# First modulation weights moved ahead of the small loads, the small loads on ScalarE's queue, and another order of the first products

## The chip, the cores and the metric

The kernel runs on one core of one Trainium2 chip. The metric is the device time of one execution in microseconds; the program is launched once and does all four layers. TensorE has two clock levels, 1.2 and 2.4 GHz; the profile gives the granted level as a share of the higher one.

## The reference, cut to what matters

Four layers of a decoder are computed for 256 prompt rows and 32 sample rows, 288 rows together, in float32. Each sub-layer's input is modulated by a shift and a scale per sequence, which come from a product of the condition vectors with a weight of 1024 x 6144 per layer. Layer 0 begins with the gated MLP mixer.

```python
    sc = jax.nn.silu(c)
    for i in range(DEPTH):
        mod = sc @ prm['w_ada'][i] + prm['b_ada'][i]
        sh1, sc1, g1, sh2, sc2, g2 = jnp.split(mod[:, None, :], 6, axis=-1)
        h = x * (1 + sc1) + sh1
        if kind == 0:
            out, v_rows = chunk_mlp_mixer(h, prm['a_w_in'][j], ...)   # z = gelu(h @ w_in)
        x = layer_norm(ALPHA * x + g1 * out, prm['ln1_g'][i], prm['ln1_b'][i])
```

So nothing of layer 0 can be multiplied with its first weight before the condition rows, the first third of `w_ada[0]` and the rows of x are there.

## The kernel before, in words

Activations lie transposed, as eight slices of 128 features x 288 rows. Each float32 product is made of three products of a rounded high part and a low part (`mm3`: Hi x hi at L294, Hi x lo at L295, Lo x hi at L297), so every weight is split on its way: ScalarE copies the high part (`hi`, L240), VectorE subtracts it (`lo`, L241), both 1024 columns at a time. Weights stream from HBM through five 1 MB buffers (`raw`); `set_plan` holds the order of the loads, `advance` and `reach` issue the next load as soon as a buffer is free, and `pump_` splits. A scheduler of the language then sets the order on each engine from the program's text, its priorities and the `issue_after` fences. Every engine executes its list strictly in that order.

The start of the program, which the change touches, goes in these steps (`setup`):

- Eight small loads on SyncE's queue (SP): the condition rows `crow` (two loads), constants `con` (identity and a selection matrix), biases `vb` (two), the prompt rows `xr` (two of 512 KB) and the sample rows `xs`. Then come the first loads of the plan. A load's completion is counted on one of eight semaphores, handed out in turn over the loads of all hardware queues, so a load waits until the eighth load before it has landed. GpSimd's queue (POOL) issues ten further small loads at the same time (`late_loads`).
- Transposes on TensorE: `crow` (L399), `vb` (L405, L406), then x slice by slice (two of `xr` at L413, one of `xs` at L414), copied out of PSUM by VectorE (L415). The SiLU of the condition is `scT`.
- The first third of the modulation in two halves (`ada_first`, g = 0 and 1). A half has four weight tiles of 1 MB, each in two loads of 512 KB and each worth four matmuls with 512 columns (L558). Each matmul writes another 32 rows of one PSUM bank. Then ScalarE copies the bank (L564, `adas`), TensorE gathers it with four small matmuls (L567), and VectorE adds the bias and makes the shift B and the scale A (L572, L573).
- `h_stream` makes Hi and Lo of four slices per half (ScalarE L705 and L708, VectorE L706 to L714).
- The first four output tiles of the value half of `a_w_in` are accumulated together (`run_units` with `inter`): for each of the eight slices k, twelve matmuls over the four tiles. `s.after(k + 1)` holds the products of slice k until a certain modulation matmul has been issued; the list `paced` holds the last matmul of g = 0 and then one for each of the four tiles of g = 1.

Of the kernel before, what the change touches and what calls it, by code (L numbers as in the profile page):

```python
# [56 lines left out]
class Net:  # L57
# [256 lines left out]
    def run_units(s, keys, x, evac, m0=0, nk=8, inter=False, kgroups=1, quiet=False):  # L314

        npair = len(keys) // kgroups
        done = 0
        pair = 0
        if inter:
            ks = keys[:2]  # L320
            ws = [s.get(k) for k in ks]
            pss = [s.psmm() for _ in range(4)]
            for k in range(nk):
                if k < nk - 1:
                    for part in range(2):
                        for m in range(4):
                            with s.after(k + 1):
                                s.mm3(pss[m][:, :T], s.wtile(ws[m // 2], k, m % 2), x(k), k == 0, False, (part,))
                    continue
                for m in range(4):  # L330
                    with s.after(k + 1):
                        s.mm3(pss[m][:, :T], s.wtile(ws[m // 2], k, m % 2), x(k), False, True)
                    if m % 2:
                        s.wfree(ks[m // 2])
                    evac(m0 + m, pss[m])
            s.paced = []
            pair = 2
        while pair < npair:
            if quiet and pair == npair - QPAIR:
                s.quiet = bool(QUIET)  # L340
            pss = [s.psmm() for _ in range(2)]
            for g in range(kgroups):
                key = keys[pair * kgroups + g]
                w = s.get(key)
                for m in range(2):
                    for k in range(nk):
                        s.mm3(pss[m][:, :T], s.wtile(w, k, m), x(g * nk + k), g == 0 and k == 0,
                              g == kgroups - 1 and k == nk - 1)
                    if m == 1:
                        s.wfree(key)  # L350
                    if g == kgroups - 1:
                        evac(m0 + pair * 2 + m, pss[m])
            pair += 1


    def setup(s):
        nc, I = s.nc, s.I
        c = s.cst
        ncst = I["consts"].shape[1]
        s.con = c.tile([128, ncst], F32, name="con")  # L360
        o = CONST_OFF
        cv = lambda k: s.con[:, o[k][0]:o[k][0] + o[k][1]]
        s.cv = cv
        s.id = cv("ident")
        s.onesD = cv("onesD")
        s.ones128 = cv("ones128")
        s.scT = c.tile([128, 8, 32], F32, name="scT")
        s.modT = [c.tile([128, 48, 9], F32, name=f"modT{i}") for i in range(2)]
        s.vT1 = c.tile([128, 128], F32, name="vT1")
        s.vT2 = c.tile([128, 128], F32, name="vT2")  # L370
        s.bT = c.tile([128, 192], F32, name="bT")
        s.X0 = s.acp.tile([128, NCH, T], F32, name="Z", tag="Z")
        s.AX = s.acp.tile([128, NCH, T], F32, name="AX")
        s.Hi = s.acp.tile([128, NCH, T], R32, name="Hi")
        s.Lo = s.acp.tile([128, NCH, T], R32, name="Lo")
        s.A = [s.acp.tile([128, 8, 9], F32, name=f"A{i}") for i in range(2)]
        s.B = [s.acp.tile([128, 8, 9], F32, name=f"B{i}") for i in range(2)]
        i0 = s.layers[0]
        with s.tc.tile_pool(name="ld", bufs=1) as ld:
            crow = ld.tile([9, D], F32, name="crow")  # L380
            vb = [ld.tile([96, 128], F32, name=f"vb{i}") for i in range(2)]
            xr = [ld.tile([128, D], F32, name=f"xr{i}") for i in range(2)]
            xs = ld.tile([32, D], F32, name="xs")

            nc.sync.dma_start(crow[0:1, :], I["c_prompt"])
            nc.sync.dma_start(crow[1:9, :], I["c_sample"])
            nc.sync.dma_start(s.con[:, :146], I["consts"][:, :146])
            bsrc = I["b_ada"].rearrange("l (c p) -> (l c) p", p=128)
            for i in range(2):
                nc.sync.dma_start(vb[i], bsrc[96 * i:96 * i + 96, :])  # L390
            for i in range(2):
                nc.sync.dma_start(xr[i], I["x_prompt"][0, 128 * i:128 * i + 128, :])
            nc.sync.dma_start(xs, I["x_sample"].rearrange("b t d -> (b t) d"))
            s.advance()

            nc.vector.memset(s.scT, 0.0)
            pt = s.psx()
            for k in range(8):
                nc.tensor.transpose(pt[:, 9 * k:9 * k + 9], crow[:, 128 * k:128 * k + 128], s.id[:9, :9])  # L399
            sg = s.wrk.tile([128, T], F32, name="sg", tag="hf", bufs=4)  # L400
            s.act(sg[:, :72], pt[:, :72], AF.Sigmoid)
            nc.vector.tensor_tensor(s.scT[:, :, :9], sg[:, :72].rearrange("p (k n) -> p k n", k=8),
                                    pt[:, :72].rearrange("p (k n) -> p k n", k=8), op=OP.mult)
            pt = s.psx()
            nc.tensor.transpose(pt[:, 0:96], vb[0], s.id[:96, :96])  # L405
            nc.tensor.transpose(pt[:, 96:192], vb[1], s.id[:96, :96])  # L406
            nc.vector.tensor_copy(s.bT, pt[:, :192])

            each = s.h_stream(s.X0, 0)
            for ch in range(NCH):  # L410
                pt = s.psx()
                for i in range(2):
                    nc.tensor.transpose(pt[:, 128 * i:128 * i + 128], xr[i][:, 128 * ch:128 * ch + 128], s.id)  # L413
                nc.tensor.transpose(pt[:, 256:288], xs[:, 128 * ch:128 * ch + 128], s.id[:32, :32])  # L414
                nc.vector.tensor_copy(s.X0[:, ch, :], pt[:, :T])  # L415
            for g in range(2):
                s.ada_first(i0, g)
                for ch in range(4 * g, 4 * g + 4):
                    each(ch)
                if g == 0:  # L420
                    s.late_loads()

# [1434 lines left out]
```

## Time and profile before

| | before |
|---|---|
| median of 3 runs | 1615.36 us (1612.78 to 1615.41) |
| the profiled execution, its own time | 1613.43 us |
| its span | 1611.7 us |
| TensorE matmul busy | 1566.9 us (97%) |
| VectorE, ScalarE busy | 1025.4 us (64%), 798.8 us (50%) |
| DMA | 332.60 MB, mean 206 GB/s |

The profile is of one execution. Its span is the time between the first and the last instruction; 1.7 us of that execution's own time lie around it. Matmuls are pipelined, so a busy TensorE is not a TensorE at its peak. Times in the trace count from the span's start.

### The profile page before, as it was taken

To read this page: it belongs to the slowest core of one execution; us is meant where nothing else is said; L and a number is where in the kernel's file an instruction comes from. 1 tells how busy PE (TensorE), PEld (TensorE's weight loads), DVE (VectorE), ACT (ScalarE), POOL (GpSimd) and SP (SyncE) were. 2 spreads that over 40 slices of the span, in tenths; PEclk is the share of its full clock that TensorE was granted. 3 is DMA by queue.
4 is the path that set the end of the run, shared out by engine and by line. 5 is a ranking of instruction groups with operands and counts; after the bars stand their busy time and mean duration, and the time that the engine had idled before them with its cause. 6 is when DMAs were issued, how large, how long until landed. Compare 5 with 4: busy or idle time off the path is not lost.

```text
span 1611.7 us, 30562 instructions
## 1 busy us (share of the span) xinstructions
PE 1566.9 (97%) x12538; PEld 1399.0 (87%) x12538; DVE 1025.4 (64%) x2290; ACT 798.8 (50%) x1435; POOL 53.1 (3%) x70
## 2 busy tenths in 40 slices
PE   7999899999999999999999999999999999999997
PEld 3778699998889789999987776779999888899997
DVE  3559564557777797556586445496565785964655
ACT  2555453545777656345354444455354463653542
POOL 1000000000001000000002110000000000000000
PEclk9999999999999999999999999999999999999999
DMA  9977695557745878554565455777545675755431
GB/s 333 341 254 242 220 293 160 163 175 246 227 142 163 276 277 280 166 174 159 162 230 186 144 184 212 259 268 240 172 157 173 245 236 192 230 191 176 157 106 43
DMA packets 222718, 332.60 MB, mean 206 GB/s; under 512 B 7171, under 2 KB 196041, under 8 KB 213362
## 3 DMA queue, kind: packets, MB, share of 16 engines
q1 hardware_dynamic: 215954, 299.86, 55.7%
q0 software_dynamic: 6624, 30.78, 5.7%
q8 instruction: 99, 1.62, 0.4%
q14 instruction: 41, 0.34, 0.1%
HBM read 324.09 MB, written 6.53 MB: 205 GB/s over the span
## 4 chain that ended last, share of the span: by engine, by line
PE 87%; DVE 6%; DMA 4%; ACT 2%; issue 1%; SPq 0%; POOL 0%; DVEq 0%; ACTq 0%; POOLq 0%
PE mm L294 23%; PE mm L297 23%; PE mm L295 22%; PE ada L504 3%; PE mm L1456 2%; DMA raw<-in_ffn_w 1%; DVE lo L241 1%; PE mx L1474 1%; PE mm L1510 1%; DVE Z L674 1%; PE mx L1528 1%; DMA raw<-in_a_w_in 1%; PE mx L863 1%; PE mx L1478 1%; PE mx L965 1%
## 5 line engine op out<-in xcount | busy, mean ns | idle before, releaser
L241 DVE TENSOR_TENSOR lo<-raw,hi 128x1024 fp32r<-128x1024 f32 x360 | 433.5, 1220 | 179.2 <-ACT hi L240 179.0
L240 ACT ACTIVATE hi<-raw 128x1024 fp32r<-128x1024 f32 x360 | 371.1, 1052 | 268.4 <-PE mm L297 194.2
L294 PE MATMUL mm<-Hi,hi 128*128 128x288 f32 x1064 | 316.5, 301 | 10.2 <-ACT hi L240 6.2
L295 PE MATMUL mm<-Hi,lo 128*128 128x288 f32 x1064 | 314.5, 299 | 0.5 <-DVE lo L241 0.4
L297 PE MATMUL mm<-FL,hi 128*128 128x288 f32 x1024 | 303.6, 297 | 0.0
L294 PE MATMUL mm<-FH,hi 128*128 128x288 f32 x1024 | 302.6, 296 | 0.0
L295 PE MATMUL mm<-FH,lo 128*128 128x288 f32 x1024 | 298.6, 292 | 0.0
L297 PE MATMUL mm<-Lo,hi 128*128 128x288 f32 x1064 | 296.4, 297 | 0.0
L294 PEld LDWEIGHTS mm<-Hi,hi 128*128 128x128 f32 x1064 | 200.1, 188 | 30.8 <-issue 10.9
L294 PE MATMUL mm<-OH,hi 128*128 128x288 f32 x704 | 206.6, 298 | 1.4 <-ACT OH L705 1.2
L295 PE MATMUL mm<-OH,lo 128*128 128x288 f32 x704 | 205.7, 296 | 0.5 <-DVE lo L241 0.5
L295 PEld LDWEIGHTS mm<-Hi,lo 128*128 128x128 f32 x1064 | 200.4, 188 | 5.9 <-issue 2.5
L297 PEld LDWEIGHTS mm<-Lo,hi 128*128 128x128 f32 x1064 | 193.9, 189 | 6.7 <-issue 5.9
L295 PEld LDWEIGHTS mm<-FH,lo 128*128 128x128 f32 x1024 | 195.2, 191 | 0.0
L297 PE MATMUL mm<-OL,hi 128*128 128x288 f32 x704 | 195.1, 295 | 0.0
L294 PEld LDWEIGHTS mm<-FH,hi 128*128 128x128 f32 x1024 | 192.4, 188 | 0.0
L297 PEld LDWEIGHTS mm<-FL,hi 128*128 128x128 f32 x1024 | 191.9, 187 | 0.0
L294 PEld LDWEIGHTS mm<-OH,hi 128*128 128x128 f32 x704 | 131.8, 187 | 6.9 <-issue 3.4
L784 ACT ACTIVATE r<-mm 128x288 f32<-128x288 f32 x128 | 52.0, 411 | 169.3 <-PE mm L297 163.7
L295 PEld LDWEIGHTS mm<-OH,lo 128*128 128x128 f32 x704 | 132.2, 188 | 1.7 <-issue 0.8
L297 PEld LDWEIGHTS mm<-OL,hi 128*128 128x128 f32 x704 | 128.0, 188 | 1.0 <-issue 0.8
L786 DVE TENSOR_TENSOR s<-r 128x288 f32<-128x288 f32 x128 | 57.7, 455 | 99.6 <-ACT r L784 99.4
(434 smaller groups left out, 2043.7 us busy)
## 6 DMA issues: line engine op xcount, KB each, us to landing
raw<-in_ffn_w SPq DMA_DIRECT2D x128, 1024.0 KB, 5.5
raw<-in_w_ada SPq DMA_DIRECT2D x88, 1024.0 KB, 6.6
raw<-in_a_w_in SPq DMA_DIRECT2D x16, 1024.0 KB, 7.8
raw<-in_b_w_in SPq DMA_DIRECT2D x16, 1024.0 KB, 5.8
raw<-in_w_ada SPq DMA_DIRECT2D x16, 512.0 KB, 9.8
raw<-in_a_w_out SPq DMA_DIRECT2D x8, 1024.0 KB, 7.9
St<-in_state_hgrn POOLq DMA_DIRECT2D x8, 512.0 KB, 5.7
out_hs_s<-St POOLq DMA_DIRECT2D x8, 512.0 KB, 4.4
```

The lines of the kernel that those rows point to most:

```text
L240: nc.scalar.activation(hi[:, a:b], r[:, a:b], AF.Copy)
L241: nc.vector.tensor_tensor(lo[:, a:b], r[:, a:b], hi[:, a:b].bitcast(F32), op=OP.subtract)
L294: mm(out, w[0], x[0], start=first, stop=False)
L295: mm(out, w[1], x[0], start=False, stop=False)
L297: s.last_mm = mm(out, w[0], x[1], start=False, stop=last).ins
L504: nc.tensor.matmul(s.pa[32 * j:32 * j + 32, :], x, w, start=(k == 0), stop=(k == last), skip_group_check=True)
L674: sub = lambda c: nc.vector.tensor_tensor(Z[:, c, :], Z[:, c, :], pm[:, :T], op=OP.subtract)
L784: nc.scalar.activation(r, ps[:, :T], AF.Relu)
L786: nc.vector.tensor_tensor(sq, r, r, op=OP.mult)
L863: nc.tensor.matmul(pt[:, 128 * q:128 * q + 128], vt01[:, q, sl], s.wsT[:, c, :], start=True, stop=True)
L965: mm(pt[32 * b:32 * b + 32, 64 * hh + 32 * g:64 * hh + 32 * g + 32], k[:, hh, a:a + 32], q[:, hh, a:a + 32], start=True, stop=True, skip_g ...
L1456: tr(pt[:, 128 * n:128 * n + 128], lat[b][t // 8][:, t % 8, 128 * c:128 * c + 128], s.id)
```

## The change

The first loads of the plan (`s.advance()`) are issued on SP before anything else, and the eight small loads go to ScalarE's queue. While g = 0 is prepared, splitting is held back (`quiet`), but for two pieces of 1024 columns that are asked for by hand after slices 0 and 2. `s.after(k)` takes the place of `s.after(k + 1)`, so the products of slice k may stand one modulation matmul earlier. Later lines move by seven: what is L558 before is L565 after, L567 is L574, L413 and L414 are L414 and L415, L705 is L712.

```diff
                     for part in range(2):
                         for m in range(4):
-                            with s.after(k + 1):
+                            with s.after(k):
                                 s.mm3(pss[m][:, :T], s.wtile(ws[m // 2], k, m % 2), x(k), k == 0, False, (part,))
                     continue
                 for m in range(4):
-                    with s.after(k + 1):
+                    with s.after(k):
                         s.mm3(pss[m][:, :T], s.wtile(ws[m // 2], k, m % 2), x(k), False, True)
...
-            nc.sync.dma_start(crow[0:1, :], I["c_prompt"])
-            nc.sync.dma_start(crow[1:9, :], I["c_sample"])
-            nc.sync.dma_start(s.con[:, :146], I["consts"][:, :146])
+            s.quiet = True
+            s.advance()
+            nc.scalar.dma_start(crow[0:1, :], I["c_prompt"])
+            nc.scalar.dma_start(crow[1:9, :], I["c_sample"])
+            nc.scalar.dma_start(s.con[:, :146], I["consts"][:, :146])
             bsrc = I["b_ada"].rearrange("l (c p) -> (l c) p", p=128)
             for i in range(2):
-                nc.sync.dma_start(vb[i], bsrc[96 * i:96 * i + 96, :])
+                nc.scalar.dma_start(vb[i], bsrc[96 * i:96 * i + 96, :])
             for i in range(2):
-                nc.sync.dma_start(xr[i], I["x_prompt"][0, 128 * i:128 * i + 128, :])
-            nc.sync.dma_start(xs, I["x_sample"].rearrange("b t d -> (b t) d"))
-            s.advance()
+                nc.scalar.dma_start(xr[i], I["x_prompt"][0, 128 * i:128 * i + 128, :])
+            nc.scalar.dma_start(xs, I["x_sample"].rearrange("b t d -> (b t) d"))
...
             for g in range(2):
+                s.quiet = g == 0
                 s.ada_first(i0, g)
                 for ch in range(4 * g, 4 * g + 4):
                     each(ch)
+                    if g == 0 and ch in (0, 2):
+
+                        s.reach(s.wlist[0])
+                        s.pump_(True)
+                s.quiet = False
```

The order of the instructions differs in the first 560 or so of TensorE's, the first 50 of ScalarE's and the first 36 of VectorE's; behind that all lists are the same. Three places matter.

The first place is the very start of ScalarE's list after the change, with the semaphores that each instruction waits for (DMAHW numbers the eight load semaphores):

```order
L387 DMA crow<-in_c_prompt 1x1024
L388 DMA crow<-in_c_sample 8x1024
L389 DMA con<-in_consts 128x146
L392 DMA vb_97<-in_b_ada 96x128
L392 DMA vb_98<-in_b_ada 96x128
L394 DMA xr_99<-in_x_prompt 128x1024 [waits DMAHW0_49]
L394 DMA xr_100<-in_x_prompt 128x1024 [waits DMAHW2_49]
L395 DMA xs<-in_x_sample 32x1024 [waits DMAHW4_49]
L281 ACT_TABLE_LOAD
L281 ACTIVATE sg<-mx 128x72 [waits PE_49]
```

Before, this list began with the table load. The semaphores now alternate between the two queues; on SP the fourth 512 KB load of `w_ada` waits for the first to land, the fifth for the second and the sixth for the third, where before the eight waited for the eight small loads.

The second place is TensorE's list from the third-last slice of x to the end of g = 0. Before:

```order
L414 MATMUL mx<-con,xs 128x32
L558 MATMUL ada<-raw,scT 32x512
L413 MATMUL mx<-con,xr_99 128x128
L413 MATMUL mx<-con,xr_100 128x128
L414 MATMUL mx<-con,xs 128x32
L413 MATMUL mx<-con,xr_99 128x128
L413 MATMUL mx<-con,xr_100 128x128
L414 MATMUL mx<-con,xs 128x32
L558 MATMUL ada<-raw,scT 32x512 x15
L567 MATMUL mx<-con,adas 128x18 x4
```

And after the change, where one more matmul of the half stands by itself behind slice 2, further up:

```order
L414 MATMUL mx<-con,xr_99 128x128
L414 MATMUL mx<-con,xr_100 128x128
L415 MATMUL mx<-con,xs 128x32
L565 MATMUL ada<-raw,scT 32x512 x4
L414 MATMUL mx<-con,xr_99 128x128
L414 MATMUL mx<-con,xr_100 128x128
L415 MATMUL mx<-con,xs 128x32
L414 MATMUL mx<-con,xr_99 128x128
L414 MATMUL mx<-con,xr_100 128x128
L415 MATMUL mx<-con,xs 128x32
L565 MATMUL ada<-raw,scT 32x512 x11
L574 MATMUL mx<-con,adas 128x18 x4
```

The sixteen matmuls of g = 0 stand as 1 and 15 before and as 1, 4 and 11 after.

The third place is TensorE's list around the end of g = 1. Before, six products of slice 3 stand ahead of the small gathering matmuls and six behind them; then slice 4 begins:

```order
L558 MATMUL ada<-raw,scT 32x512 x4
L294 MATMUL mm<-Hi,hi 128x288
L295 MATMUL mm<-Hi,lo 128x288
L294 MATMUL mm<-Hi,hi 128x288
L295 MATMUL mm<-Hi,lo 128x288
L294 MATMUL mm<-Hi,hi 128x288
L295 MATMUL mm<-Hi,lo 128x288
L567 MATMUL mx<-con,adas 128x18 x4
L445 MATMUL mx<-con,v_259 128x128
L446 MATMUL mx<-con,v_260 128x128
L294 MATMUL mm<-Hi,hi 128x288
L295 MATMUL mm<-Hi,lo 128x288
```

After the change all 48 products of slices 0 to 3 are done when the last modulation matmul is, and the row behind the two transposes is already of slice 4:

```order
L565 MATMUL ada<-raw,scT 32x512 x2
L297 MATMUL mm<-Lo,hi 128x288 x3
L565 MATMUL ada<-raw,scT 32x512 x2
L574 MATMUL mx<-con,adas 128x18 x4
L452 MATMUL mx<-con,v_253 128x128
L453 MATMUL mx<-con,v_254 128x128
L294 MATMUL mm<-Hi,hi 128x288
```

The first products moved the other way: before, the first four matmuls of g = 1 stand ahead of them; after, six products of slice 0 stand ahead of those four matmuls. On ScalarE the first split (L240) now stands between `adas` and the first Hi, where before all four splits stood behind the four slices' Hi and hf.

## Rows read from the trace of the kernel before

**Rows 1.** The page: span, busy time of each engine, one costly group.
```profile
span 1611.7 us, 30562 instructions
PE 1566.9 (97%) x12538; PEld 1399.0 (87%) x12538; DVE 1025.4 (64%) x2290; ACT 798.8 (50%) x1435; POOL 53.1 (3%) x70
L241 DVE TENSOR_TENSOR lo<-raw,hi 128x1024 fp32r<-128x1024 f32 x360 | 433.5, 1220 | 179.2 <-ACT hi L240 179.0
```

**Rows 2.** Chain that ended last, 0 to 60 us: start us, us, what.
```profile
3.37 5.66 DMA xr<-in_x_prompt
...
24.62 0.60 ACT Hi L705
```

**Rows 3.** Timeline of SP's queue: start us, us, what it issues.
```profile
0.81 0.35 SPq L385 DMA_DIRECT2D crow<-in_c_prompt  x1
...
3.84 0.43 SPq L393 DMA_DIRECT2D xs<-in_x_sample  x1
4.31 6.09 SPq L142 DMA_DIRECT2D raw<-in_w_ada  x8
```

**Rows 4.** DMA issues in the stretch 2.55 to 3.05: KB, us to landing.
```profile
xr<-in_x_prompt SPq DMA_DIRECT2D x1, 512.0 KB, 4.4
vb<-in_b_ada SPq DMA_DIRECT2D x1, 48.0 KB, 3.4
...
v<-in_ln_b POOLq DMA_DIRECT2D x1, 16.0 KB, 3.3
```

**Rows 5.** DMA issues in the stretches 3.55 to 4.0 and 5.51 to 6.0.
```profile
xr<-in_x_prompt SPq DMA_DIRECT2D x1, 512.0 KB, 5.7
xs<-in_x_sample SPq DMA_DIRECT2D x1, 128.0 KB, 5.9
...
v<-in_ln_b POOLq DMA_DIRECT2D x1, 16.0 KB, 5.7
...
v<-in_b_lb POOLq DMA_DIRECT2D x1, 16.0 KB, 6.1
```

**Rows 6.** Busy time by stretch: last columns are clock, DMA share, GB/s.
```profile
2.00:3.00 1.00, 0.00 (x0) 0.00 (x0) 0.00 (x0) 0.10 (x1) 1.00 (x3) 1.00 0.57 136
...
4.00:5.00 1.00, 1.00 (x9) 0.97 (x9) 0.00 (x0) 0.08 (x1) 1.00 (x3) 1.00 0.44 83
...
11.00:14.00 3.00, 3.00 (x10) 1.34 (x10) 1.81 (x5) 0.00 (x0) 0.00 (x0) 1.00 1.05 387
...
27.70:31.00 3.30, 2.88 (x8) 0.40 (x8) 2.27 (x4) 3.30 (x5) 0.00 (x0) 0.50 1.05 387
```

**Rows 7.** Timeline of TensorE, 12 to 24 us.
```profile
13.34 1.92 PE L558 MATMUL ada<-raw,scT 128*32 128x512 f32 x2
15.19 0.69 PE L413 MATMUL mx<-con,xr 128*128 128x128 f32 x2
...
16.05 0.69 PE L413 MATMUL mx<-con,xr 128*128 128x128 f32 x2
...
16.91 5.57 PE L558 MATMUL ada<-raw,scT 128*32 128x512 f32 x30
```

**Rows 8.** TensorE groups in 0 to 20.5, 28 to 31, 31.2 to 42.
```profile
L558 PE MATMUL ada<-raw,scT 128*32 128x512 f32 x22 | 6.2, 1023 | 0.0
L558 PE MATMUL ada<-raw,scT 128*32 128x512 f32 x8 | 3.1, 1047 | 3.9 <-DMA raw<-in_w_ada 3.9
L558 PE MATMUL ada<-raw,scT 128*32 128x512 f32 x26 | 6.3, 636 | 0.0
```

**Rows 9.** Timeline of TensorE, 36 to 46 us.
```profile
38.27 1.05 PE L558 MATMUL ada<-raw,scT 128*32 128x512 f32 x4
39.26 0.40 PE L294 MATMUL mm<-Hi,hi 128*128 128x288 f32 x1
...
42.04 0.40 PE L294 MATMUL mm<-Hi,hi 128*128 128x288 f32 x1
...
45.19 0.37 PE L294 MATMUL mm<-Hi,hi 128*128 128x288 f32 x1 [0.18 <-DVE hf L710]
```

## The prediction

> **What bounds the kernel now.** I read the page first. TensorE is busy 97% of the span [rows 1], so almost everywhere its own work sets the pace, and the change leaves that work alone behind the first 560 instructions or so. What it can move is the start. Whatever the start gains or loses until TensorE runs without gaps is carried to the end one for one, because the lists behind are the same. So I followed the chain of waits through the first 60 us. It begins with the load of x: the chain stands on `xr` for 5.66 us, then runs through TensorE's transposes and the modulation matmuls into ScalarE's first Hi [rows 2]. The reader is to see that the chain goes through **x, not through the modulation weights**. `xs` is issued at 3.84 and lands 5.9 us later, at 9.7 [rows 3, 5], and from there TensorE has hardly a pause until the sixteen modulation matmuls of g = 0 end at 16.91 + 5.57 = 22.5 [rows 7]. I call that moment G. The products of slice 4, the first that need g = 1, start at 45.19 [rows 9]. From there the program is the same in both kernels, so the start of slice 4 is my yardstick.
>
> **The change, part by part.** *Issue of the weights.* They begin at 0.81 in place of 4.31, 3.5 us earlier [rows 3]. That is no gain by itself: TensorE reaches the weights behind the transposes of x, and no row there waits for a weight of g = 0 [rows 7]. I set it to zero. Its cover is x; if x came at once, the weights would be next.
>
> *Landing of x.* This is the large term. The trace has no load on ScalarE's queue, so I take the nearest: the small loads on POOL's queue, which run against SP's queue at the same time. A 16 KB load issued near 2.6 lands 3.3 us later, and SP's `vb` from the same half microsecond 3.4 later [rows 4]. Another 16 KB load lands after 5.7 us, and the 512 KB `xr` beside it after 5.7 as well; a later one still takes 6.1 [rows 5]. A load of a thirtieth of the size lands when the large one does, so the two queues **take turns load by load**, one of mine against one of yours, whatever their sizes. ScalarE's queue has eight loads: five small ones, two `xr`, then `xs`. Against each now stands a 512 KB load of weights. SP's queue does not run dry, although its fourth load waits for the first to land: two more are still queued then. So `xs` comes behind seven of the weight loads. At 387 GB/s [rows 6] one of these (524288 bytes) takes 1.35 us, seven 9.5. The three loads of x (1.18 MB) take 3.0. The small loads kept the DMA engines busy for 0.57 us between 2 and 3 and 0.44 between 4 and 5 [rows 6]; for all of them I take 1.5. Transfers start at about 2.1 (none before 2, 136 GB/s in the next microsecond). Sum: 2.1 + 9.5 + 3.0 + 1.5 = 16.1, say 16.3, against 9.7: **+6.6 us**. Bounds: 0, if ScalarE's loads lose nothing, and 8.0, if all eight weight loads go ahead. I take the value near the upper end, because the rows of POOL's queue are the only ones with two queues at once. The Trainium skill (DMA: Bandwidth & Descriptors, Issuing engines are not separate DMA queues) holds that loads from several issuing engines interleave on the same DMA engines and that a second issuer saves no more than the time to issue; by that sentence alone x would lose only its share of the bandwidth, the term would be +1.1 (the first rival) and the sum +3.3. The same page (Queues, rings and completion order) adds that an engine drains a whole packet of one queue before it turns to the next; by that the term stays at +6.6, and the trace agrees for POOL's and SP's queues, while no run here shows ScalarE's. The table load on ScalarE comes behind the eight issues and the condition's transposes behind `con`; both end long before 16.3, so I cost them at zero.
>
> *The order of the sixteen matmuls.* At this point TensorE runs at its lower level. The granted column holds 1.00 here, but the durations decide: L558 takes 1023 ns on average before 20.5, as in the stretch with 0.50 granted (1047), and 636 where 1.00 is granted later [rows 6, 8]. Up to four neighbours of these matmuls run side by side, so one alone costs as much as a group. The single one took 15.19 - 13.34 = 1.85 us [rows 7]. Before: 1.85 + 5.57 = 7.4, the last part of it at the full level. After, as 1, 4 and 11: 1.85 + 1.85 + three groups of 1.7 to 1.85, say 5.3, sum 9.0: **+1.6 us**. The six slices of x in between cost 0.86 each in either order (16.05 - 15.19). Bounds: -0.6, if the level rises ahead of the eleven and halves them (2.2 less), and 1.8.
>
> *From G to slice 4.* Before: 45.19 - 22.5 = 22.7. After, three edits go together. The early split puts the first products before the matmuls of g = 1. Hi begins 2.1 behind G as before [rows 2], then lo (1.2 [rows 1]) and the first Lo follow, so I estimate that the matmuls of g = 1 start at G + 5.0, where before they waited 3.9 us for weights [rows 8] and started at G + 5.6: -0.6. Those weights are now early, since G is late. Then TensorE has the first four together (1.0), six pairs at 0.99 (39.26 - 38.27 [rows 9]), 42 products at about 0.134 (5.6) and some 1.0 for going back and forth: 13.5. The last piece, from the end of g = 1 to slice 4, is 45.19 - 42.04 = 3.15 [rows 9]. It held twelve products before and holds none now, which is what `s.after(k)` gives back of its gain. Sum at the full level 5.0 + 13.5 + 3.15 = 21.7. The pause behind G lets the level fall as it did before (0.50 in 27.70:31.00 [rows 6]). That cost about 2 us then (3.1 for the four matmuls in place of 1.0 [rows 8, 9]); I take 1.6, between 0 and 3.3. Result 23.3: **+0.6 us**, bounds -1.0 and +2.3.
>
> Sum: 6.6 + 1.6 + 0.6 = +8.8 us. Against the profiled execution's own time this is 1613.43 + 8.8 = 1622.2; the median of the runs lies 1.9 above that execution, and from there it is 1624.2. I forecast **1623.2**, between the two, slower by 0.5%. A measurement of this kernel can tell about 0.2% (3.2 us) from no change. The likeliest case by itself runs from 1620.5 to 1627.5.
>
> **The rivals.** *Even sharing, no turns.* If the two hardware queues share bandwidth by bytes, `xr` and `xs` lose only what runs beside them: 3.0 us of transfer at half speed from about 4.8 ends at 10.8, +1.1 in place of +6.6. Then the sum is 1.1 + 1.6 + 0.6 = +3.3, and with the lower bounds of the last two terms -0.5: no change mostly, about 1616.5 from the median. For it: SP's and ScalarE's loads are both issued in hardware, POOL's by software. Against it: [rows 4, 5].
>
> *Faster: x untouched and the full level early.* If ScalarE's loads get through as quickly as SP's did, `xs` lands at 9.7 and the early weights let TensorE reach its full level before the first L558. Six slices at 0.86 and ten half-groups at 0.5 end at about 20; with 21.7 behind it slice 4 starts at 41.7, 3.5 us early: 1611.9. It decides at the level around 14 us. Against it: TensorE was already busy 3.00 of 3.00 us from 11 to 14 [rows 6] and was still slow at 16.91.
>
> *The start is not carried to the end*, or its terms cancel: if a later wait on a DMA or on ScalarE already sets the pace, the shift vanishes there; 1615.4. Against it: 97% busy TensorE.
>
> **How the numbers follow.** Turns 0.57, all of it slower. Even sharing 0.25: 0.07 slower, 0.18 within 0.2%. The faster rival 0.11. No net shift 0.07. So slower 0.64, same 0.25, faster 0.11. The range starts at 1613.2, which leaves out the faster rival and takes in even sharing and no shift with the run's own spread, and ends at 1627.6, the sum with its upper bounds (8.0 + 1.8 + 2.3 = 12.1 on the median), so that little is left above.
>
> **What would show it.** Right: `xs` lands near 16 and TensorE's transposes of x end 5 us or more later than before; the eleven L565 take over 4.5 us; no TensorE product lies between the last L574 and slice 4, a gap of 1 us or more; slice 4 starts near 54. Wrong: `xs` lands before 12, or slice 4 starts before 48. If slice 4 is late but the time is not, the carrying to the end was the wrong step.

## The result and the profile after

The changed kernel takes 1624.37 us (median of six runs, 1622.24 to 1631.89), the kernel before it 1615.28 us in the runs beside it: a ratio of **1.0072** (95% interval 1.0057 to 1.0088). The ratio is taken over the single runs; the quotient of the two medians is 1.0056. A later set of runs, e15 below, gave 1.0052 (1.0031 to 1.0074). The change makes the kernel slower by some 0.6%. Runs of one kernel scatter by half a per cent here, so below about 0.15% a ratio says nothing.

The profiled execution took 1622.33 us, 8.9 more than that of before. From the page, span and busy time:

```profile
span 1620.4 us, 30559 instructions
PE 1570.6 (97%) x12538; PEld 1402.1 (87%) x12538; DVE 1025.8 (63%) x2290; ACT 799.7 (49%) x1435; POOL 53.4 (3%) x70
```

TensorE's busy share is that of before, 97% [rows 1]; it is busy 3.7 us longer, and the span is 8.7 us longer. The chain that ended last, 0 to 60 us (start us, us, what):

```profile
0.81 0.53 ACTq L387
...
1.69 6.17 DMA con<-in_consts
7.88 6.70 DMA xs<-in_x_sample
14.62 0.42 PE mx L415 x2
...
23.54 2.74 PE ada L565 x22
```

Before, the chain began with `xr` [rows 2]. Now it stands on **`con` and then on `xs`**, one behind the other. The timelines of the two issuing queues say why:

```profile
0.81 9.71 SPq L142 DMA_DIRECT2D raw<-in_w_ada  x8
```

```profile
1.69 0.44 ACTq L389 DMA_DIRECT2D con<-in_consts  x1
2.16 1.12 ACTq L392 DMA_DIRECT2D vb<-in_b_ada  x2
3.32 2.04 ACTq L394 DMA_DIRECT2D xr<-in_x_prompt  x2
7.88 0.33 ACTq L395 DMA_DIRECT2D xs<-in_x_sample  x1
8.24 1.28 ACT L281 ACT_TABLE_LOAD   x1 [8.24 <-DMA con<-in_consts]
```

`con` is issued at 1.69 and lands at 7.86; before it landed at 3.76. `xs` is the eighth load after `con` in the common count of the eight semaphores (its instruction waits for DMAHW4, which `con` holds), so ScalarE could issue it only at 7.88. It lands at 14.58, where before it landed at 9.7 [rows 3, 5]. The eight weight loads took until 10 us to be issued, because each from the fourth on waited for one ahead of it to land.

TensorE's timeline, 14 to 32 us (start us, us, what, in brackets idle time before it and what ended it):

```profile
14.62 0.42 PE L415 MATMUL mx<-con,xs 32*128 32x32 f32 x2 [0.41 <-DMA xs<-in_x_sample]
...
15.83 1.92 PE L565 MATMUL ada<-raw,scT 128*32 128x512 f32 x2
...
20.26 1.94 PE L565 MATMUL ada<-raw,scT 128*32 128x512 f32 x8
...
22.92 0.44 PE L414 MATMUL mx<-con,xr 128*128 128x128 f32 x2
...
23.47 2.77 PE L565 MATMUL ada<-raw,scT 128*32 128x512 f32 x22
26.95 1.07 PE L574 MATMUL mx<-con,adas 128*128 128x18 f32 x8 [0.71 <-ACT adas L571]
```

These rows answer to [rows 7]. G, the end of the sixteen, is 23.47 + 2.77 = 26.24, 3.8 later than before. The eleven took 2.77 us, because the higher level came just ahead of them: at 22.92 two transposes of x take 0.44 us, where at 15.19 in [rows 7] they took 0.69. Then TensorE around the end of g = 1:

```profile
48.24 1.05 PE L565 MATMUL ada<-raw,scT 128*32 128x512 f32 x4
50.05 1.07 PE L574 MATMUL mx<-con,adas 128*128 128x18 f32 x8 [0.76 <-ACT adas L571]
...
52.36 0.37 PE L294 MATMUL mm<-Hi,hi 128*128 128x288 f32 x1 [0.98 <-DVE hf L717]
...
54.42 0.44 PE L294 MATMUL mm<-Hi,hi 128*128 128x288 f32 x1
...
57.14 0.29 PE L294 MATMUL mm<-Hi,hi 128*128 128x288 f32 x1
```

Two idle stretches of 0.76 and 0.98 us stand where before twelve products lay and 0.18 us were idle [rows 9]. Slice 4 starts at 52.36, 7.2 later than before. Soon after it a product takes 0.44 us in place of 0.29. Busy time by stretch (last columns: granted clock, DMA share, GB/s):

```profile
29.60:39.80 10.20, 9.40 (x30) 4.05 (x30) 6.34 (x14) 5.68 (x9) 0.00 (x0) 0.50 1.03 362
39.80:52.00 12.20, 10.82 (x62) 6.05 (x58) 0.84 (x6) 1.11 (x3) 0.00 (x0) 1.00 1.03 359
53.50:56.90 3.40, 3.40 (x17) 3.40 (x16) 3.33 (x14) 3.40 (x7) 1.40 (x1) 0.50 0.86 277
```

The lower level lasts 10.2 us behind G, where before it lasted about 3.4 (27.70 to 31.00 in [rows 6]), and it comes back for 3.4 us right behind the pause. So the 8.7 us of this execution are: `xs` +4.9; the sixteen and the transposes among them -1.1; G to slice 4 +3.4 (26.1 in place of 22.7); behind slice 4 +1.5.

### The profile page after: what moved, and what is told of

Its sections match the earlier page's. It is cut to its first block, busy times and chain, and to the rows that moved or that the text cites. A ratio compares the mean times of both kernels' runs of the same rounds, so it can differ in the third digit from the quotient of the medians.

```text
span 1620.4 us, 30559 instructions
## 1 busy us (share of the span) xinstructions
PE 1570.6 (97%) x12538; PEld 1402.1 (87%) x12538; DVE 1025.8 (63%) x2290; ACT 799.7 (49%) x1435; POOL 53.4 (3%) x70
## 4 chain that ended last, share of the span: by engine, by line
PE 88%; DVE 6%; DMA 3%; ACT 2%; issue 1%; POOL 0%; DVEq 0%; ACTq 0%
PE mm L294 23%; PE mm L297 23%; PE mm L295 23%; PE ada L511 3%; PE mm L1463 2%; DMA raw<-in_ffn_w 1%; PE mx L1481 1%; DVE lo L241 1%; PE mm L1517 1%; PE ada L565 1%; DVE Z L681 1%; PE mx L1535 1%; PE mx L870 1%; PE mx L1485 1%; PE mx L972 1%
## 5 line engine op out<-in xcount | busy, mean ns | idle before, releaser
L240 ACT ACTIVATE hi<-raw 128x1024 fp32r<-128x1024 f32 x360 | 371.4, 1052 | 264.3 <-PE mm L297 194.3
```

Source lines behind the costliest of these rows:

```text
L240: nc.scalar.activation(hi[:, a:b], r[:, a:b], AF.Copy)
```

## Experiments

The change has three parts that can be undone one at a time: **loads** (weights first on SP, small loads on ScalarE's queue), **split** (`quiet` and the two early pieces) and **fences** (`s.after(k)`). In the table "xs" is its landing, G and slice 4 as in the prediction, all in us from the profile of the run. An empty cell is as before, "0 to 2" is the new fence for these slices alone; e5, e6 and e7 follow further down. Each ratio is to the runs of the kernel before that stand beside it; their medians lie between 1613.4 and 1615.9.

| run | loads | split | fences | xs | G | slice 4 | median | ratio to before (95%) |
|---|---|---|---|---|---|---|---|---|
| before | | | | 9.7 | 22.5 | 45.2 | 1615.3 | 1 |
| changed kernel | new | new | new | 14.6 | 26.2 | 52.4 | 1624.4 | 1.0072 (1.0057 to 1.0088) |
| e15, the same | new | new | new | 14.8 | 28.8 | 53.1 | 1622.5 | 1.0052 (1.0031 to 1.0074) |
| e1 | | new | new | 10.1 | 22.7 | 48.0 | 1620.3 | 1.0050 (1.0036 to 1.0065) |
| e2 | new | | | 14.5 | 28.5 | 51.4 | 1620.1 | 1.0042 (1.0028 to 1.0056) |
| e3 | | new | | 10.4 | 22.7 | 46.6 | 1614.3 | 0.9996 (0.9981 to 1.0011) |
| e4 | | | new | 9.7 | 22.2 | 51.1 | 1619.7 | 1.0041 (1.0027 to 1.0056) |
| e10 | new | new | | 14.7 | 28.5 | 53.3 | 1620.3 | 1.0033 (1.0015 to 1.0051) |
| e12 | new | new | 0 to 2 | 14.8 | 26.8 | 48.1 | 1618.6 | 1.0025 (1.0007 to 1.0043) |
| e13 | | new | 0 to 2 | 9.9 | 22.9 | 46.5 | 1616.1 | 1.0010 (0.9995 to 1.0024) |
| e14 | | | 3 alone | 9.8 | 21.7 | 47.5 | 1616.5 | 1.0010 (0.9996 to 1.0023) |

**The parts.** e1 is the changed kernel with the loads back:

```diff
-            s.advance()
-            nc.scalar.dma_start(crow[0:1, :], I["c_prompt"])
...
+            nc.sync.dma_start(crow[0:1, :], I["c_prompt"])
...
+            s.advance()
```

> Only the loads are undone: the eight small loads stand on SP's queue again, ahead of the weights; the early split and the new order of the products stay. Theory A (x comes late because ScalarE's loads take turns with 512 KB loads of weights): the sample rows land at 9.7 us as before, g = 0 ends at 22 to 23.5, slice 4 starts at 44 to 46.5, time 1613 to 1617. Rival B (the new order of matmuls and products is what costs): the sample rows land at 9.7 but slice 4 still starts after 50 and the time stays at 1620 or more.

e2 makes the move of the loads alone, in the kernel before:

```diff
-            nc.sync.dma_start(crow[0:1, :], I["c_prompt"])
...
+            s.advance()
+            nc.scalar.dma_start(crow[0:1, :], I["c_prompt"])
...
-            s.advance()
```

> The kernel before with only the loads moved: weights first on SP, the eight small loads on ScalarE's queue, old splits and old product order. Theory A: the sample rows land at 14 to 15 us, slice 4 starts 4 to 7 us later than 45.2, time 1619 to 1625. Rival B: the loads alone change nothing, slice 4 within 1.5 us of 45.2, time 1614 to 1617.

e4 is the kernel before with `s.after(k)` alone:

```diff
-                            with s.after(k + 1):
+                            with s.after(k):
```

> The kernel before with only the fence of the products moved by one. On TensorE this leaves the products in their old order but splits the sixteen matmuls of g = 0 into 1, 4 and 11. Theory A: the sample rows land at 9.7; g = 0 ends 0.5 to 1.8 us later than 22.5, slice 4 starts 0.5 to 2 us later, time 1615.5 to 1617.5. Rival B: 3 us or more later, time 1618 or more.

That text has a premise that was wrong: e4 keeps the sixteen as 1 and 15; only the products' places move.

e3 is the changed kernel with loads and fences back, so the split alone (the move of e1, and this):

```diff
-                            with s.after(k):
+                            with s.after(k + 1):
```

> The loads are back on SP's queue and the fences are s.after(k + 1) again; of the change only the held-back splitting with its two early pieces is left. Theory A (the cost of the order lies in the fences: with s.after(k) no product is left to fill the pause before slice 4, and the clock falls behind that pause): six products stand in the pause again, no stretch at half level begins within 3 us behind the start of slice 4, slice 4 starts at 45 to 46.5, and the time is within 0.2% of before. Theory B (the early split itself costs, because ScalarE and VectorE make the first Hi and hf later): the first Hi is late, slice 4 starts at 47.5 or later as in the run with the loads back, and the time is 0.3% or more above before.

e10 is the changed kernel with that second edit alone, only the fences back:

> The changed kernel with s.after(k + 1) in place of s.after(k); loads on ScalarE's queue and the early split stay. Theory A (fences cost through the empty pause): xs lands at 14.6 and the sixteen matmuls end near 26 as in the changed kernel, six products stand in the pause before slice 4, slice 4 starts at 50 to 51.5 in place of 52.36, no half-level stretch begins right behind it, and the time is 1619 to 1622, some 3 us under the changed kernel. Theory C (only the loads cost, the fences nothing once the start is late): slice 4 at 52 or later and the time within 1.5 us of the changed kernel's 1624.4.

e2 came as expected: `xs` at 14.5, slice 4 6.2 later, and +0.42% (6.6 us between the medians). But e1 missed its 1613 to 1617: without the loads the rest still costs 0.50%, and its slice 4 at 48.0 fits neither theory. e3 clears the split (0.9996, six products in the pause again, slice 4 at 46.6) and e4 puts a cost on **the fences, +0.41% alone**. e10 met the time of its theory A, 1620.3 in place of 1624.4, but not its slice 4: in that trace the level rose only at 27.5 and G came at 28.5. The interval of e10 lies below that of the changed kernel's first set, but meets that of e15. The profiled executions of e1 and e3 are not typical ones: e1's is the fastest of its five (1614.40), e3's the slowest of its twelve (1619.77). So the traces show orders and waits here, and the ratios show the cost. The traces also show where the order of the sixteen comes from: they stand as 1, 4 and 11 in e2 and e10, and as 1 and 15 in e1, e3 and e4. It goes with the loads, and not, as the expectation of e4 had it, with the fences.

So there are two costs, 0.42 for the loads and 0.41 for the fences, and -0.04 for the split, each alone in the kernel before. That their sum of 0.79 stands near the 0.72 and 0.52 of the whole proves little, for e4 has a wait that the changed kernel has not. Putting back the loads alone is clear in e3 against e10 (0.9996 and 1.0033), but not in e1 against the changed kernel (1.0050 against 1.0072 and 1.0052) nor in e13 against e12 below (1.0010 and 1.0025).

TensorE at G in e4:

```profile
22.91 1.06 PE L567 MATMUL mx<-con,adas 128*128 128x18 f32 x8 [0.71 <-ACT adas L564]
29.38 0.85 PE L294 MATMUL mm<-Hi,hi 128*128 128x288 f32 x2 [5.41 <-ACT hi L240]
```

The products of slice 0 stand ahead of the first four matmuls of g = 1, and without the early split they wait 5.4 us for it. The matmuls of g = 1 then start 9.2 us behind G, where before it was 5.6 and in the changed kernel 5.3.

**Which fence.** Twelve products in the pause before slice 4, six on either side of the gathering matmuls, are the difference that the fence of slice 3 makes. e12 is the changed kernel with this fence back:

```diff
-                            with s.after(k):
+                            with s.after(k + 1 if k == 3 else k):
```

> The changed kernel with the fence of slice 3 alone as before (k + 1), so that six products stand in the pause before slice 4 again; slices 0 to 2 keep s.after(k), so six products of slice 0 still stand ahead of the first four matmuls of g = 1. If the empty pause is what the new fences cost: no half-level stretch begins right behind the start of slice 4, and the time is 1619 to 1621.5, as with all fences back (1620.3). If the products ahead of the first matmuls of g = 1 cost it (the list on TensorE is held by a split that is late): the half-level stretch behind the sixteen matmuls lasts 10 us as in the changed kernel, and the time stays at 1623 to 1625.

e13 makes the same edit in e1, so with the loads back on SP:

> The loads back on SP's queue, the early split kept, and of the new fences only those of slices 0 to 2: the fence of slice 3 is k + 1. With all fences new the time was 1620.3, with all of them back 1614.3. If the empty pause is the cost: slice 4 starts within 1 us of 47, no half-level stretch right behind it, 1613 to 1616.5. If the products ahead of the first matmuls of g = 1 are the cost: 1618.5 or more.

TensorE of e12 at the same place:

```profile
45.85 1.02 PE L574 MATMUL mx<-con,adas 128*128 128x18 f32 x8
46.72 0.30 PE L452 MATMUL mx<-con,v 128*128 128x128 f32 x1
46.86 0.27 PE L453 MATMUL mx<-con,v 128*128 128x128 f32 x1
46.89 0.38 PE L294 MATMUL mm<-Hi,hi 128*128 128x288 f32 x1
...
48.10 0.37 PE L294 MATMUL mm<-Hi,hi 128*128 128x288 f32 x1 [0.17 <-DVE hf L717]
```

The first products of slice 4 in e1, then in e13:

```profile
48.04 0.37 PE L294 MATMUL mm<-Hi,hi 128*128 128x288 f32 x1 [0.98 <-DVE hf L717]
```

```profile
46.52 0.37 PE L294 MATMUL mm<-Hi,hi 128*128 128x288 f32 x1 [0.18 <-DVE hf L717]
```

The pause is 0.17 and 0.18 in place of 0.98, and the 0.76 ahead of L574 is gone too. No stretch at the lower level follows right behind it in e12 or e13; e12's median of 1618.6 is a little better than expected, e13's 1616.1 is as expected. This one fence takes the ratio from 1.0072 and 1.0052 to 1.0025, and with the loads back from 1.0050 (e1) to 1.0010 (e13). The interval of e12 meets that of e15, but not that of the first set, and those of e1 and e13 do not meet. The fences of slices 0 to 2 then cost nothing that can be measured: e12 stands beside e10 (1.0025, 1.0033), e13 beside e3 (1.0010, 0.9996). So of the fences the one of slice 3, which empties the pause, is the deciding one, as long as the early split is there.

e14 tries the emptied pause by itself, in the kernel before. Its fence for slice 3 stands one matmul earlier than in the changed kernel (`s.after(2)` in place of `s.after(3)`), and one product stays in the pause:

```diff
-                            with s.after(k + 1):
+                            with s.after(2 if k == 3 else k + 1):
```

> The kernel before with the fence of slice 3 alone moved forward (after the third of the five matmuls on the list): five of the six products that stood between the gathering matmuls and slice 4, and the six ahead of them, are done before; one product is left behind the gathering matmuls. Loads, split and the other fences are those of before. If the emptied pause is a cost by itself: a gap of about 1 us ahead of slice 4, slice 4 1 to 2 us later than 45.19, and 1616.5 to 1621. If it costs only together with the fences of slices 0 to 2: within 0.1% of before, 1614 to 1617.

```profile
46.32 0.38 PE L297 MATMUL mm<-Lo,hi 128*128 128x288 f32 x1
47.54 0.37 PE L294 MATMUL mm<-Hi,hi 128*128 128x288 f32 x1 [0.84 <-DVE hf L710]
```

The gap is there (0.84), slice 4 comes 2.3 later, and the time is up by 0.10% (-0.04 to 0.23): that is 1.6 us, with an interval from -0.6 to 3.7. A cost of the idle time's size fits, and none fits too. It neither shows nor refutes the cost alone.

**The level.** e15 is the changed kernel once more:

> The changed kernel once more, for a second trace of the same lists. If the half-level stretches belong to the order: 10 us of half level again behind the sixteen matmuls and 3.4 us right behind the start of slice 4, slice 4 within 0.5 us of 52.36. If the first stretch's length is chance: it is 3.4 or 6.8 us, slice 4 starts at 49 to 51.5, while the gap of 1 us ahead of slice 4 stays. xs lands at 14.4 to 14.8 either way.

```profile
24.05 4.74 PE L565 MATMUL ada<-raw,scT 128*32 128x512 f32 x22
```

```profile
31.50:38.30 6.80, 6.20 (x21) 3.44 (x21) 6.03 (x16) 6.33 (x11) 0.00 (x0) 0.50 0.83 291
...
53.50:56.90 3.40, 3.40 (x28) 3.40 (x27) 2.87 (x18) 3.40 (x7) 0.00 (x0) 1.00 1.14 327
```

With the same lists the eleven took 4.74 us in place of 2.77, the lower level lasted 6.8 in place of 10.2, and the one behind the pause did not come at all. The gap before slice 4 was 0.97 again, slice 4 at 53.05, the span 1620.7 against 1620.4. So **the length of a stretch at the lower level differs between executions of the same lists**, which I call chance; the gap and the landing of `xs` repeat. The expectation's chance branch held in the stretches, not in slice 4, since the later G ate what the shorter stretch gave.

**The queue.** e5 is the changed kernel with the loads of the modulation weights halved (256 KB each):

```diff
-                s.nc.sync.dma_start(tv[:, :, h, :], src[:, :, h, :])
+                for two in range(2):
+                    s.nc.sync.dma_start(tv[:, two, h, :], src[:, two, h, :])
```

> The changed kernel with each weight load of w_ada cut in two of 256 KB. Turns load by load: con stands behind three loads of half the size, so it moves from 3.5 to 4.5 on and lands at 5.5 to 6.3 in place of 7.86, the small loads and x follow earlier, xs lands at 11.5 to 13.5 in place of 14.58, and the time is 1 to 4 us under the changed kernel's 1624.4. If what delays con is something else (the start of ScalarE's queue, or sharing by packets and not by loads), con lands at 7.3 or later, xs at 14 or later, and the time stays within 1.5 us of 1624.4.

e6 is the changed kernel with x ahead of `crow` and `vb` on ScalarE's queue:

```diff
-            nc.scalar.dma_start(crow[0:1, :], I["c_prompt"])
-            nc.scalar.dma_start(crow[1:9, :], I["c_sample"])
             nc.scalar.dma_start(s.con[:, :146], I["consts"][:, :146])
...
             nc.scalar.dma_start(xs, I["x_sample"].rearrange("b t d -> (b t) d"))
+            nc.scalar.dma_start(crow[0:1, :], I["c_prompt"])
+            nc.scalar.dma_start(crow[1:9, :], I["c_sample"])
...
```

> The changed kernel with another order on ScalarE's queue: con, the two xr, xs, and only then crow and vb; the weights still come first on SP's queue. Turns load by load: xs is the fourth load of its queue and is issued at once, no load's landing stands ahead of it, so it lands at 10 to 11.5 in place of 14.58; con lands at 4.5 to 5.5. The condition now comes last and is the new wait: the sixteen matmuls cannot begin before crow has landed and its SiLU is made (about 2.5 us behind), so they end at 23.5 to 25.5 and the time is 1620 to 1623. If x was late only because of the shared semaphores, xs lands under 9.5 here. If x does not matter for the end, the time stays at 1624.

e7 is the kernel before with the three loads of x on ScalarE's queue, `con` first on SP's, and the weights still behind the small loads:

```diff
...
+            nc.sync.dma_start(s.con[:, :146], I["consts"][:, :146])
+            nc.scalar.dma_start(xr[0], I["x_prompt"][0, 0:128, :])
             nc.sync.dma_start(crow[0:1, :], I["c_prompt"])
...
+            nc.scalar.dma_start(xs, I["x_sample"].rearrange("b t d -> (b t) d"))
...
-                nc.sync.dma_start(xr[i], I["x_prompt"][0, 128 * i:128 * i + 128, :])
-            nc.sync.dma_start(xs, I["x_sample"].rearrange("b t d -> (b t) d"))
```

> The kernel before with the loads of x on ScalarE's queue and the five small ones on SP's queue, both ahead of the weights. Theory A (a queue is slowed by what large loads the other queue holds ahead): nothing large stands against x at first, the sample rows land at 7 to 9 us, slice 4 starts 0.5 to 2.5 us earlier than 45.2, time 1612.5 to 1615. Rival C (loads issued by ScalarE are slow by themselves): the sample rows land after 11, slice 4 after 46.5, time 1616.5 or more.

From the DMA issues, first of e5, then of e6 (KB, us to landing):

```profile
con<-in_consts ACTq DMA_DIRECT2D x1, 73.0 KB, 5.0
```

```profile
xs<-in_x_sample ACTq DMA_DIRECT2D x1, 128.0 KB, 9.7
```

In e5 `con` landed at 6.73, between the two theories: 1.1 us earlier with loads of half the size, where turns alone would give 2. `xs` came later (15.1), for now twice as many loads share the eight semaphores and it was issued at 9.96 only. The time was 1630.5, a ratio of 1.0091 (1.0068 to 1.0114), the worst of all and far from both expected times; what makes it so slow stays open. In e6 `xs` needs no landing, is issued at 2.33 and lands at **12.04**, a little above the 10 to 11.5 expected. Yet the time is 1625.0 (1.0061; 1.0037 to 1.0085), above the 1620 to 1623 expected. The time alone could mean that x does not matter; the trace shows that the wait moved on. TensorE of e6:

```profile
14.46 0.99 PE L400 MATMUL mx<-con,crow 9*128 9x9 f32 x8 [14.46 <-DMA crow<-in_c_sample]
16.55 0.42 PE L406 MATMUL mx<-con,vb 96*128 96x96 f32 x1 [1.09 <-DMA vb<-in_b_ada]
...
18.08 0.42 PE L407 MATMUL mx<-con,vb 96*128 96x96 f32 x1 [0.69 <-DMA vb<-in_b_ada]
```

The transposes of `crow` and `vb` stand ahead of x on TensorE's list, and now these loads are last. G is 31.8; I had seen the wait for `crow` and not the one for `vb`. In e7 `xs` lands at 8.5, 1.2 earlier than before, so a load is not slow because ScalarE issues it; slice 4 starts at 44.7, 0.5 earlier. The time missed its 1612.5 to 1615: it is 1617.6, a ratio of 1.0022 (1.0007 to 1.0037), and the trace does not say where that comes from. No version was faster than before; e3, e13 and e14 cannot be told from it.

## Why the prediction came out as it did

The forecast of 1623.2 lies 1.2 under the median, and the sum of +8.8 beside the 8.9 of the profiled execution. The direction held, and so did the main step, that x comes late because of the weights; how it comes late, and the single terms, held less well, so that the sum fits this closely is luck.

*Issue of the weights, zero.* Held. No L565 of g = 0 waits for a weight, in any run with the loads moved.

*Landing of x, +6.6.* x came late behind the weights, but **the size was off: +4.9** (e2 by itself +4.8). The step that failed is "SP's queue does not run dry", and with it "`xs` comes behind seven of the weight loads". SP's loads wait for landings from the fourth on, so only four had landed when `xs` did (at 4.93, 6.30, 9.11 and 14.40). What SP's queue (q1) had moved by 14.58, then both queues between 8 and 9 us (packets, MB, share of 16 engines):

```profile
q1 hardware_dynamic: 1329, 2.58, 54.4%
```

```profile
q10 hardware_dynamic: 142, 0.30, 96.1%
...
q1 hardware_dynamic: 21, 0.02, 7.2%
```

2.58 MB are 4.9 weight loads in place of seven, and for a microsecond SP's queue moved next to nothing. With 4.9 my sum gives 2.1 + 6.6 + 3.0 + 1.5 = 13.2. The other 1.4 us are about the rate: all queues together moved 4.24 MB in the 12.5 us from 2.1 on, 340 GB/s in place of 387. ScalarE's queue also stood until 7.88 for the landing of `con`, a wait that I had printed and not costed; what it costs is not shown, since the prompt rows, issued ahead of `xs`, were still under way (TensorE waits for `xr` until 13.52). The sum of the prediction was also rounded up from 16.1 to 16.3.

"Take turns load by load" was half right. It fits the start, but once loads of both queues are under way they go packet for packet (last section). The packets are of 2 to 4 KB, so turns by packets, on which the prediction leaned, are not turns by loads. The rival of even sharing (`xs` at 10.8) fell by its number, and so did the faster one. The Trainium skill (DMA: Bandwidth & Descriptors, Issuing engines are not separate DMA queues) says that loads of several issuing engines interleave and that another issuer saves only issue time. The trace agrees with the interleaving (169 packets against 166 between 9.5 and 12 us). That `con` landed 4.1 us later through the other queue does not speak against the second part, for two weight loads are now issued ahead of it; what the issuer alone adds, no run here shows.

*Order of the sixteen, +1.6.* It comes with the loads (1, 4 and 11 in e2 as well, without the other two parts). Measured: -1.1 in one trace, +1.2 in the other (G +6.3, of which `xs` 5.1). The step "three groups of 1.7 to 1.85, say 5.3" was 4.74 in e15 and 2.77 in the first trace, where the level rose just ahead of the eleven. My lower bound of -0.6 was too narrow for it.

*G to slice 4, +0.6.* **This was mis-sized: +3.4 and +1.5.** At the full level I had 21.7. Measured, less half of the stretch at the lower level, it is 26.1 - 5.1 = 21.0 and 24.25 - 3.4 = 20.9, and before it was 22.7 - 1.7 = 21.0. So the piece is as long as before, and in both traces the level makes the difference. The term that failed is the level, "I take 1.6, between 0 and 3.3": it was 5.1 and 3.4. "It held twelve products before and holds none now" was right, but I booked it as a piece of 3.15 that stays as long. The products lay in time that TensorE must wait anyway; moved ahead of it, the idle time came on top, 0.76 + 0.98 - 0.18 = 1.6 us. In e12, with the products back, the piece is 21.3 - 1.7 = 19.6, and the time comes down by more than that.

*From slice 4 to the end, nothing.* +1.5 and +1.2. Behind slice 4 the stretches at the lower level, without the last one, in which TensorE has nothing left to do, add up to 17.1 us before, 20.5 in the first trace and 13.7 in e15. So the level fits the +1.5, and the +1.2 of e15 stays open. A single trace does not carry the start to the end one for one: in e3 slice 4 is 1.5 later and the span 6.4 longer, in e1 2.9 and 1.0.

Expected signs: the transposes of x end 6.6 us later (right, 5 or more); the eleven over 4.5 us (2.77, then 4.74); a gap of 1 us or more (0.98, 0.97); slice 4 near 54 (52.4, 53.1); `xs` near 16 (14.6). The total was right in part because a term too large for x stood against one too small for the fences.

What stays open: the medians fall by 4 to 6 us with the fence of slice 3, and the idle time explains 1.6. For the rest there is the mean granted clock of each execution. Span times this clock is a rough estimate of the time without the lower level (rough, because TensorE also waits at that level, and because the start counts as full there); the rest of the span is what the lower level takes. Without it the kernel before takes 1599 to 1600 us in each of the four sets of runs beside the experiments, the changed kernel 1606 and 1604, e2 1604, e10 1605, e12 1602, e3 1599 and e1 and e13 1598. So by this estimate the loads cost 4 to 8 us in each pair of kernels that differ in them alone. The lower level takes 12 to 14 us before, 17 in the changed kernel and 15 in e12, 20 in e1 and 16 in e13. So it makes up 3 of the 4 us between e1 and e13, and about 3 of the 5 to 7 between the changed kernel and e12. It also makes up nearly all that e7 loses (15 against 12 beside it). That an emptied pause makes the lower level likelier is argued, not shown: e1, e4 and the first trace have a stretch at 0.50 right behind it, e5, e6, e14 and e15 have none, and in e14 the level takes no more than before (13 against 14).

## What to carry to other kernels

Moving loads to a second queue is not only a matter of who issues them: see which loads of the other queue are issued ahead, what they move meanwhile, and follow the shared load semaphores to see when each can be issued at all. When a fence is loosened, look at what lay behind it: work that filled an unavoidable wait costs nothing there and leaves a hole when it is moved forward. A sum that comes out right can hold two wrong terms, so test the parts by themselves.

## What the runs showed unexpectedly

Two queues share the DMA engines in two ways, one after the other. From the changed kernel's DMA view, packets of each queue in the stretches 2.5 to 3.5, 5 to 7.5 and 9.5 to 12 us (q1 is SP's queue, q10 ScalarE's; packets, MB, share of 16 engines):

```profile
q1 hardware_dynamic: 145, 0.30, 90.9%
```

```profile
q1 hardware_dynamic: 297, 0.58, 65.2%
...
q10 hardware_dynamic: 215, 0.11, 16.6%
```

```profile
q10 hardware_dynamic: 169, 0.61, 64.0%
q1 hardware_dynamic: 166, 0.34, 36.6%
```

At first only weights move, though `crow` and `con` had been issued at 1.37 and 1.69 on ScalarE's queue: at the start they stand behind the weight loads issued before them. In e6, where `con` is issued at 0.82 beside the first weights, ScalarE's queue moves 65 packets in the same stretch. Once loads of both queues are under way they go packet for packet, 169 against 166, and then the queue with the larger packets gets the more bytes (0.61 against 0.34 MB). That fits the half-size loads of e5, which moved `con` by 1.1 us and not by 2; no run tests it by itself.

The same lists gave G at 26.24 and 28.79 in two executions, and spans that differ by 0.3 us. G moves by 2.55 us with the moment at which the level rises, and the start of slice 4, which I had taken for a yardstick, by 0.7; medians over many runs decide, not one trace.
